# Delta-net mixer: squared norms of queries and keys as column sums on TensorE

## The chip, the cores and the metric

The kernel runs on one core of a Trainium2 chip. Five engines with queues of their own work side by side: TensorE (PE, with its weight loads listed apart as PEld), VectorE (DVE), ScalarE (ACT), GpSimd (POOL) and SyncE (SP), which here issues DMAs. The metric is the device time of one execution in microseconds; less is better.

## What is computed

The program is a trunk of two layers. Layer 0 mixes with a gated delta net and layer 1 with retention, and each has a convolutional feed-forward block behind it. The change is in the delta net alone. There are 8 heads with 128 features each, 1024 tokens, chunks of 64 tokens in the reference.

```python
qkv = jax.nn.silu(causal_dwconv(qkv, conv_w))
q, k, v = jnp.split(qkv, [H * dk, 2 * H * dk], axis=-1)
q = _l2norm(_chunk_heads(q, H, C)) * (dk ** -0.5)      # x * rsqrt(sum(x*x) + 1e-6)
k = _l2norm(_chunk_heads(k, H, C))
...
kb = k * beta[..., None]
kk = jnp.where(strict, jnp.einsum('bhncd,bhnmd->bhncm', kb, k) * decay, 0.0)
...
sol = lax.linalg.triangular_solve(kk + eye, rhs, left_side=True, lower=True, unit_diagonal=True)
...
qk = jnp.where(causal, jnp.einsum('bhncd,bhnmd->bhncm', q, k) * decay, 0.0)
...
o = o * lax.rsqrt(jnp.mean(o * o, axis=-1, keepdims=True) + 1e-6) * norm_w
```

So each token of each head needs the sum over 128 features of q squared and of k squared. The kernel never scales q and k themselves: the norm of k goes into the factors `cj` (beta over the squared norm) and `ir` (the norm), and the norm of q goes into the epsilon of the output's normalization.

## The kernel before

**Tiles.** Features lie on partitions. A tile of queries, keys or values (`feats[ti]`, with ti 0 to 7 for queries, 8 to 15 for keys, 16 to 23 for values of one head) is two halves of 128 features x 512 tokens, which take two of the 20 buffers named qkv. The kernel works in chunks of 128 tokens, eight for a head. Heads go in four pairs.

**Who fills TensorE.** In the delta-net stage, generators (`filler`, `t_path`, `t_chain`, `prep`, `dt_half`, `scan`, `tail`) yield work, and `run` chooses among them by priority with a clock of planned times: `pm` and `ptr` add a planned cost for each product, and the table `LAT` says how long after a step its result is reckoned to be there. The order on TensorE that comes out is fixed at build time (`pq` pins it). `filler` has the lowest priority: it makes the projections, 48 products of 128x512 for each half tile (`mm3` in three terms, `hT` against `wh` and `wl`), with the convolution and Silu behind them (`conv_half`, lines 446 to 459). When a tile is ready, an event `("f", ti)` is emitted at a planned time, and other streams wait for it.

**Norms of queries.** `ssq_late` starts `LAT["ssq"]` after a query tile's projections: `ssq_tile` transposes its eight 128x128 blocks on TensorE into banks of the pool acc (line 473), and ScalarE squares each block with a running sum (line 476). Line 478 adds the epsilon.

**Norms of keys.** `t_path` makes, for each head and half, four Gram blocks k k^T in one bank of the pool mm. The squared norms are their diagonals: VectorE multiplies each block with the unit matrix and sums (line 776), then adds the epsilon (779), inverts (780), multiplies by beta (781), and scales the blocks into U (line 786). After the second half POOL takes the square root `ir` (line 783). U then goes to the solve by columns on VectorE (lines 794 to 811), and from there through `t_chain` to `scan`.

**Pools.** PSUM has four banks acc, two banks mm (`mm_tile`, for all that is short-lived) and two banks sc (for the scan). A bank of mm that isn't read yet stops TensorE at the next request but one. The buffers `cv` (four) serve the convolution and the squares. Values are scaled by `ir` in `prep` (line 913), query-key blocks by the decay in `dt_half` (line 948), and `scan` scales by `cj` (line 976).

The units of `bg_ada` (lines 206 to 234), which load modulation weights (mvw) and accumulate them on VectorE (line 216), are done one at a time between the projections.

Of the kernel before, what the change touches and what calls it, by code (L numbers as in the profile page):

```python
# [15 lines left out]
P = 128  # L16
# [17 lines left out]
def trunk_kernel(ctx: ExitStack, tc, A):  # L34
# [8 lines left out]
    BUFS = {"hTa": 8, "hTb": 8, "qkv": 20, "aux": 4, "auh": 8, "lane": 4, "cv": 4, "ada": 1,  # L43
            "wr": 2, "wh": 2, "wl": 2, "t2": 3, "sm": 14, "sm2": 6, "st": 8, "s8": 6, "S": 4, "qx": 3, "fs": 1, "xT": 4}

# [417 lines left out]

    def ssq_tile(ti, tr):
        o = feats[ti]
        r = ssq[ti] = ct(f"ssq{ti}", [P, NCH])
        for half in range(2):
            pt = acc_tile()
            sq = tl("cv", [P, 516], name="sq")
            for c in range(4):  # L470
                cs = slice(c * P, (c + 1) * P)
                tr(pt[:, cs], o[half][:, cs])
            for c in range(4):
                n = half * 4 + c
                cs = slice(c * P, (c + 1) * P)
                act.activation(sq[:, cs], pt[:, cs], AF.Square, accum_out=r[:, n:n + 1])
        if ti < GH:
            dve.tensor_scalar(r, r, 1e-6, 1e-6 * P, ALU.add, ALU.mult)
        else:
            dve.tensor_scalar(r, r, 1e-6, None, ALU.add)  # L480

# [267 lines left out]
    def t_path(p):  # L749
# [12 lines left out]
        for hh, h in enumerate(heads):  # L762
            yield after_ev(("f", GH + h))
            sk = tl("sm", [P, NCH], name="sk")
            cj[h] = tl("sm", [P, NCH], name="cj")
            ir[h] = tl("sm", [P, NCH], name="ir")
            for q4 in range(2):
                yield LAT["kk"]
                pt = mm_tile()
                for c in range(4):  # L770
                    ks = fx(GH + h, q4 * 4 + c)
                    pm(pt[:, c * P:(c + 1) * P], ks, ks)
                for c in range(4):
                    n = q4 * 4 + c
                    junk = tl("S", [P, P], name="jk")
                    dve.scalar_tensor_tensor(junk, pt[:, c * P:(c + 1) * P], 1.0, ident, ALU.mult, ALU.mult,
                                             accum_out=sk[:, n:n + 1])
                qs = q4s(q4)
                dve.tensor_scalar(sk[:, qs], sk[:, qs], 1e-6, None, ALU.add)
                dve.reciprocal(cj[h][:, qs], sk[:, qs])  # L780
                dve.tensor_tensor(cj[h][:, qs], cj[h][:, qs], beta[:, qs, h], ALU.mult)
                if q4:
                    pool.tensor_tensor(ir[h], sk, phalf, ALU.pow)
                for c in range(4):
                    n = q4 * 4 + c
                    dve.scalar_tensor_tensor(U[h][:, n], pt[:, c * P:(c + 1) * P], cj[h][:, n:n + 1],
                                             U[h][:, n], ALU.mult, ALU.mult)
            for b in range(4):
                bs = slice(32 * b, 32 * b + 32)
                act.activation(X[bs, :, hh * 8:hh * 8 + 8].rearrange("p i c -> p c i"), U[h][bs, :, bs], AF.Copy)  # L790
# [246 lines left out]

    def ssq_late(ti):
        yield LAT["ssq"]
        ssq_tile(ti, ptr)  # L1040
        emit(("f", ti), 1.0)

    def filler(items):
        for kind, ti in items:
            if kind == "h":
                if ti > 1:
# [4 lines left out]
                    first_out(ti, 1, acc)  # L1051
                if first[ti] < GH:
                    yield [(0.2, ssq_late(first[ti]))]
# [21 lines left out]
            if kind == "c":  # L1075
                if ti < GH:
                    yield [(0.2, ssq_late(ti))]
# [834 lines left out]
```

## Time and profile before

| what | value |
|---|---|
| timed runs, median (lowest to highest) | 3035.81 us (3035.24 to 3036.67) |
| the profiled execution, from its first to its last instruction | 3033.2 us |
| granted TensorE clock, mean over the span | 0.977 |
| delta-net stage with the projections | about 86 to 640 us of the span |
| transposes for the norms of queries (line 639, into acc) | 64 records, median 272 ns |
| Gram blocks and query-key blocks (line 636, mm<-qkv) | 256 records, median 275 ns |
| products with the unit matrix (line 776) | 64, median 286 ns |

A row of a timeline gives the start, the time from start to end in us, the engine, the line, the operation with its output and inputs, and a count of records that were merged. In square brackets stands how long the engine was idle before it and what ended that. Records of TensorE overlap, so a product's cost in a dense stretch is the distance from start to start, not its duration. A product of 128x128 blocks in full precision stands as two records, a transpose as one. A row of a line lists the least, median and longest duration in ns.

### The profile page before, as it was taken

Reading aid. Unit: us, or ns where it says so; the run is one execution under the profiler, and the core shown is the slowest. Engines: PE = TensorE matmul, PEld = TensorE weight load, DVE = VectorE, ACT = ScalarE, POOL = GpSimd, SP = SyncE. Lnnn points to the kernel's source line nnn. Section 1 sums busy time; section 2 is a strip of 40 time slices with the busy share of each in tenths; the row PEclk is TensorE's granted clock in tenths of the full one; section 3 lists DMA queues with packets and bytes.
Section 4 is the critical chain, followed back from the end, with each engine's and each line's share of the span. In section 5 each row is a group of like instructions: output and inputs, shape, how many; then the busy total and the mean of one; then the engine's idle time right before and its main releaser. Section 6 shows DMA issues by size and latency. Waiting matters only on the chain.

```text
span 3033.2 us, 39037 instructions
## 1 busy us (share of the span) xinstructions
PE 2841.1 (94%) x13590; PEld 2309.7 (76%) x13590; DVE 2303.6 (76%) x3971; ACT 1314.4 (43%) x2408; POOL 671.3 (22%) x637
## 2 busy tenths in 40 slices
PE   8999899999999999998999999999998899999996
PEld 7877777877778888776777787767776678887885
DVE  5878788565888888988688645666788887777988
ACT  4745555434544444535333342222344544444442
POOL 0312211043021111820023302432200011113604
PEclk9999999999999999999999999999999999999998
DMA  7231222254354445854322544656654243335663
GB/s 275 78 122 53 77 84 78 88 176 144 107 169 149 148 150 170 316 176 154 132 100 89 174 163 138 209 178 178 214 199 150 90 144 104 105 105 202 238 192 122
DMA packets 243028, 450.23 MB, mean 148 GB/s; under 512 B 22928, under 2 KB 76432, under 8 KB 242832
## 3 DMA queue, kind: packets, MB, share of 16 engines
q1 hardware_dynamic: 211648, 400.02, 40.2%
q10 hardware_dynamic: 29760, 43.00, 3.9%
q0 software_dynamic: 1424, 4.72, 0.4%
q8 instruction: 107, 1.75, 0.2%
q14 instruction: 89, 0.73, 0.1%
HBM read 339.13 MB, written 108.53 MB: 148 GB/s over the span
## 4 chain that ended last, share of the span: by engine, by line
PE 55%; DVE 22%; DMA 11%; issue 6%; ACT 4%; POOL 2%; SPq 0%; POOLq 0%; DVEq 0%; ACTq 0%
PE acc L636 11%; PE acc L1148 7%; PE acc L110 4%; PE acc L111 4%; PE acc L112 4%; PE sc L636 4%; PE sc L1148 3%; DMA mvw<-in_ada_w 2%; PE acc L278 2%; PE acc L279 2%; PE acc L280 2%; PE mm L636 2%; DMA wr<-in_ffn_up 2%; DVE qkv L457 2%; DVE wb L90 2%
## 5 line engine op out<-in xcount | busy, mean ns | idle before, releaser
L636 PE MATMUL acc<-hT,wh 128*128 128x512 f32 x960 | 299.4, 393 | 0.0
L1546 POOL TENSOR_TENSOR o<-o 128x512 f32<-128x512 f32 x88 | 118.0, 1352 | 721.5 <-DVE o L1539 680.5
L278 PE MATMUL acc<-bb,ab 128*128 128x512 f32 x504 | 190.5, 406 | 33.5 <-DVE ab L90 20.4
L1148 PE MATMUL acc<-T,wb 128*128 128x512 f32 x840 | 206.0, 393 | 10.3 <-DVE wb L90 10.0
L279 PE MATMUL acc<-bb,ab 128*128 128x512 f32 x504 | 204.5, 406 | 8.8 <-DVE bb L90 8.5
L636 PEld LDWEIGHTS acc<-hT,wh 128*128 128x128 f32 x960 | 181.8, 189 | 34.1
L89 ACT ACTIVATE ab<-ar 128x512 fp32r<-128x512 f32 x210 | 128.6, 624 | 168.0 <-PE acc L280 83.7
L636 PE MATMUL acc<-hT,wl 128*128 128x512 f32 x480 | 201.2, 419 | 0.1
L280 PE MATMUL acc<-bb,ab 128*128 128x512 f32 x504 | 200.9, 400 | 0.0
L1148 PEld LDWEIGHTS acc<-T,wb 128*128 128x128 f32 x840 | 157.9, 189 | 48.4 <-DVE wb L90 14.7
L90 DVE TENSOR_TENSOR ab<-ar,ab 128x512 fp32r<-128x512 f32 x210 | 167.9, 809 | 34.5 <-ACT ab L89 34.1
L90 DVE TENSOR_TENSOR wl<-wr,wh 128x1024 fp32r<-128x1024 f32 x85 | 108.7, 1279 | 97.2 <-ACT wh L89 96.4
L90 DVE TENSOR_TENSOR wb<-wr,wb 128x512 fp32r<-128x512 f32 x162 | 114.5, 709 | 87.7 <-ACT wb L89 85.2
L90 DVE TENSOR_TENSOR wb<-mm,wb 128x512 fp32r<-128x512 f32 x216 | 145.0, 683 | 17.5 <-ACT wb L89 15.6
L89 ACT ACTIVATE wh<-wr 128x1024 fp32r<-128x1024 f32 x101 | 106.8, 1059 | 111.2 <-PE acc L636 43.4
L89 ACT ACTIVATE wb<-mm 128x512 fp32r<-128x512 f32 x216 | 122.8, 594 | 66.6 <-DVE mm L1194 65.5
L1205 ACT ACTIVATE pc<-acc 128x512 f32<-128x512 f32 x143 | 84.4, 592 | 147.1 <-PE acc L1148 92.5
L278 PEld LDWEIGHTS acc<-bb,ab 128*128 128x128 f32 x504 | 96.9, 194 | 62.5 <-DVE ab L90 20.3
L1525 DVE SCALAR_TENSOR_TENSOR o<-g,vc,o 128x512 f32<-128x512 f32 (+2 forms) x176 | 136.6, 795 | 5.1 <-ACT o L1520 4.5
L636 PE MATMUL acc<-wh,hT 128*128 128x512 f32 x384 | 137.2, 420 | 2.0 <-DVE vv L90 2.0
L89 ACT ACTIVATE wb<-wr 128x512 fp32r<-128x512 f32 x162 | 98.8, 626 | 87.0 <-DMA wr<-in_ffn_up 47.2
L216 DVE SCALAR_TENSOR_TENSOR ada<-mvw,e,ada 128x512 f32<-128x512 f32 x140 | 107.7, 769 | 29.0 <-DMA mvw<-in_ada_w 28.7
(636 smaller groups left out, 7855.7 us busy)
## 6 DMA issues: line engine op xcount, KB each, us to landing
wr<-in_ffn_up SPq DMA_DIRECT2D x96, 512.0 KB, 4.2
mvw<-in_ada_w SPq DMA_DIRECT2D x80, 512.0 KB, 4.3
ad<-o SPq DMA_DIRECT2D x154, 256.0 KB, 2.6
ar<-ad SPq DMA_DIRECT2D x154, 256.0 KB, 4.3
Br<-in_ffn_down SPq DMA_DIRECT2D x88, 256.0 KB, 3.7
wr<-in_ret_wv SPq DMA_DIRECT2D x32, 512.0 KB, 3.6
ar<-od SPq DMA_DIRECT2D x56, 256.0 KB, 5.3
xs<-xt ACTq DMA_DIRECT2D x24, 512.0 KB, 3.9
```

Source lines behind the costliest of these rows:

```text
L89: act.activation(dst_h, src, AF.Copy)
L90: eng.tensor_tensor(dst_l, src, dst_h, ALU.subtract)
L110: mm(acc, wl[:, k], hl[0], start=first, stop=False)
L111: mm(acc, wh[:, k], hl[1], start=False, stop=False)
L112: mm(acc, wh[:, k], hl[0], start=False, stop=last)
L278: mm(acc, a[1][:, sl], w[0], start=first, stop=False)
L279: mm(acc, a[0][:, sl], w[1], start=False, stop=False)
L280: mm(acc, a[0][:, sl], w[0], start=False, stop=last)
L636: pq(pe.matmul(out, lhsT, rhs, start=start, stop=stop), cost)
L1148: return pe.matmul(*a, skip_group_check=True, **kw)
L1525: dve.scalar_tensor_tensor(tv, gv[:, c0 - j:c1 - j], w[:, 2 - j:3 - j], tv, ALU.mult, ALU.add)
L1546: pool.tensor_tensor(o[d], o[x], o[y], op)
```

## The change

`ssq_tile` now serves keys as well as queries. For each half, ScalarE squares the 128x512 features in one instruction, and TensorE multiplies each block of 128 tokens, as the stationary operand, with a single column of ones. The sum over features of each token lands in one column of a bank of the pool mm, eight columns for a tile. For a query VectorE adds the epsilon as before. For a key it adds the epsilon, inverts and multiplies by beta, and POOL takes the root, once for the whole tile. The transposes, the products with the unit matrix and the small operations in `t_path` go. Key tiles now pass through `ssq_late`, which for keys waits also for the event `("g",)` of the gates (beta must be there); so `("f", ti)` of a key is emitted later than the 2.85 us that it was planned with before. The sums get a planned cost of 0.06, and `sm` has 16 buffers in place of 14.

```diff
-            "wr": 2, "wh": 2, "wl": 2, "t2": 3, "sm": 14, "sm2": 6, "st": 8, "s8": 6, "S": 4, "qx": 3, "fs": 1, "xT": 4}
+            "wr": 2, "wh": 2, "wl": 2, "t2": 3, "sm": 16, "sm2": 6, "st": 8, "s8": 6, "S": 4, "qx": 3, "fs": 1, "xT": 4}
...
-    def ssq_tile(ti, tr):
+    def ssq_tile(ti, mm):
         o = feats[ti]
         r = ssq[ti] = ct(f"ssq{ti}", [P, NCH])
+        pt = mm_tile()
         for half in range(2):
-            pt = acc_tile()
             sq = tl("cv", [P, 516], name="sq")
+            act.activation(sq[:, 0:HALF], o[half], AF.Square)
             for c in range(4):
-                cs = slice(c * P, (c + 1) * P)
-                tr(pt[:, cs], o[half][:, cs])
-            for c in range(4):
-                n = half * 4 + c
-                cs = slice(c * P, (c + 1) * P)
-                act.activation(sq[:, cs], pt[:, cs], AF.Square, accum_out=r[:, n:n + 1])
+                mm(pt[:, half * 4 + c:half * 4 + c + 1], sq[:, c * P:(c + 1) * P], ones[:, 0:1])
         if ti < GH:
-            dve.tensor_scalar(r, r, 1e-6, 1e-6 * P, ALU.add, ALU.mult)
-        else:
-            dve.tensor_scalar(r, r, 1e-6, None, ALU.add)
+            dve.tensor_scalar(r, pt[:, 0:NCH], 1e-6, 1e-6 * P, ALU.add, ALU.mult)
+            return
+        h = ti - GH
+        dve.tensor_scalar(r, pt[:, 0:NCH], 1e-6, None, ALU.add)
+        cj[h] = tl("sm", [P, NCH], name="cj")
+        ir[h] = tl("sm", [P, NCH], name="ir")
+        dve.reciprocal(cj[h], r)
+        dve.tensor_tensor(cj[h], cj[h], beta[:, :, h], ALU.mult)
+        pool.tensor_tensor(ir[h], r, phalf, ALU.pow)
...
             yield after_ev(("f", GH + h))
-            sk = tl("sm", [P, NCH], name="sk")
-            cj[h] = tl("sm", [P, NCH], name="cj")
-            ir[h] = tl("sm", [P, NCH], name="ir")
...
-                for c in range(4):
-                    n = q4 * 4 + c
-                    junk = tl("S", [P, P], name="jk")
-                    dve.scalar_tensor_tensor(junk, pt[:, c * P:(c + 1) * P], 1.0, ident, ALU.mult, ALU.mult,
-                                             accum_out=sk[:, n:n + 1])
-                qs = q4s(q4)
-                dve.tensor_scalar(sk[:, qs], sk[:, qs], 1e-6, None, ALU.add)
-                dve.reciprocal(cj[h][:, qs], sk[:, qs])
-                dve.tensor_tensor(cj[h][:, qs], cj[h][:, qs], beta[:, qs, h], ALU.mult)
-                if q4:
-                    pool.tensor_tensor(ir[h], sk, phalf, ALU.pow)
...
     def ssq_late(ti):
+        if ti >= GH:
+            yield after_ev(("g",))
         yield LAT["ssq"]
-        ssq_tile(ti, ptr)
+        ssq_tile(ti, lambda o, l, r: pm(o, l, r, cost=0.06))
         emit(("f", ti), 1.0)
...
-                if first[ti] < GH:
+                if first[ti] < 2 * GH:
                     yield [(0.2, ssq_late(first[ti]))]
...
-                if ti < GH:
+                if ti < 2 * GH:
                     yield [(0.2, ssq_late(ti))]
```

The first place is on TensorE, early in the stage, where the last decay products of the first head pair (gm against m_lowr) lie among projections (acc from hT and the weights wl and wh); cst is the unit matrix of a transpose. Before:

```order
L636 MATMUL mm<-gm,m_lowr 128x512 x2
L636 MATMUL acc<-hT,wl 128x512
L636 MATMUL acc<-hT,wh 128x512 x2
L636 MATMUL acc<-hT,wl 128x512
L636 MATMUL acc<-hT,wh 128x512 x2
L636 MATMUL acc<-hT,wl 128x512
L636 MATMUL acc<-hT,wh 128x512 x2
L639 MATMUL acc<-cst,qkv 128x128 x8
```

And with the change, from the decay product before it on (sq are the squares, ones the column):

```order
L638 MATMUL mm<-gm,m_lowr 128x512 x2
L638 MATMUL mm<-ones,sq 128x1 x16
L638 MATMUL acc<-hT,wl 128x512
L638 MATMUL acc<-hT,wh 128x512 x2
L638 MATMUL acc<-hT,wl 128x512
L638 MATMUL acc<-hT,wh 128x512 x2
L638 MATMUL acc<-hT,wl 128x512
L638 MATMUL acc<-hT,wh 128x512 x2
L638 MATMUL mm<-gm,m_lowr 128x512 x2
L638 MATMUL acc<-hT,wl 128x512
L638 MATMUL acc<-hT,wh 128x512 x2
L638 MATMUL mm<-ones,sq 128x1 x8
```

The two key tiles of the pair come in as sixteen sums in one go, right behind a decay product, and the query tile's eight transposes become eight sums; all of them now take banks of mm.

The second place is on VectorE, where the Gram blocks of the first pair are scaled into U. Before, one half of a head:

```order
L776 SCALAR_TENSOR_TENSOR jk,sk<-mm,cst 128x128 x4
L457 SCALAR_TENSOR_TENSOR qkv<-raw,vc,qkv 128x512
L779 TENSOR_SCALAR sk<-sk 128x4
L780 RECIPROCAL cj<-sk 128x4
L781 TENSOR_TENSOR cj<-cj,beta 128x4
L786 SCALAR_TENSOR_TENSOR U<-mm,cj,U 128x128 x4
```

With the change, both heads' factors, which stand ahead of all four halves:

```order
L477 TENSOR_SCALAR ssq_988<-mm 128x8
L216 SCALAR_TENSOR_TENSOR ada<-mvw,e,ada 128x512
L480 RECIPROCAL cj<-ssq_988 128x8
L481 TENSOR_TENSOR cj<-cj,beta 128x8
L477 TENSOR_SCALAR ssq_1008<-mm 128x8
L480 RECIPROCAL cj<-ssq_1008 128x8
L481 TENSOR_TENSOR cj<-cj,beta 128x8
```

The products with the unit matrix are gone, the three small operations are done once for a head, and behind them the scaling (now line 774) follows its Gram blocks directly.

## Prediction

> **What bounds the kernel now.** I read the page's totals first, then the busy time by stretches, then the list of who waited for whom. The delta-net stage, the only one that the change touches, runs from about 86 us to 640 us. The next rows give each engine's busy time with its count of instructions, in the order PE, weight loads (PEld), DVE, ACT, POOL, and then the granted clock.
>
> ```profile
> PE 2841.1 (94%) x13590; PEld 2309.7 (76%) x13590; DVE 2303.6 (76%) x3971; ACT 1314.4 (43%) x2408; POOL 671.3 (22%) x637
> ...
> 86.00:206.00 120.00, 120.00 (x565) 100.11 (x564) 100.43 (x224) 77.41 (x151) 33.63 (x47) 1.00 0.32 102
> 206.00:282.00 76.00, 65.50 (x546) 56.43 (x545) 51.89 (x173) 30.24 (x59) 16.18 (x18) 0.89 0.21 75
> 282.00:640.00 358.00, 334.37 (x2366) 284.14 (x2365) 258.94 (x665) 188.74 (x438) 63.28 (x102) 0.98 0.27 87
> ```
>
> Up to 206 us TensorE never stops: 120.00 of 120.00. From there to 640 us it stands for 10.5 + 23.6 = 34.1 us (76 - 65.50 and 358 - 334.37), at a clock that is sometimes halved: 0.89 over 76 us and 0.98 over 358 us mean 0.11 x 76 + 0.02 x 358 = 15.5 us of lost clock. VectorE is at 84% in the first stretch and about 70% later. So the stage is bound by TensorE's work, with a pool of 34.1 + 15.5 = 49.6 us that could be won back. What fills the pool is in the list of TensorE's waits (us in total, times, longest):
>
> ```profile
> PE mm L639 <- DVE DT L948: 9.4, 5, 3.5
> PE sc L636 <- ACT w L976: 7.7, 7, 1.8
> PE mm L636 <- DVE qkv L913: 3.7, 2, 3.1
> PE sc L636 <- DVE Sn L984: 3.6, 5, 1.7
> PE acc L639 <- ACT qkv L458: 2.4, 1, 2.4
> PE mm L636 <- DVE U L786: 1.7, 3, 1.0
> PE sc L636 <- DVE u L971: 1.7, 4, 0.6
> ```
>
> The largest, 9.4 + 3.7 us, are PSUM banks of the pool mm that TensorE wants again while VectorE is late in reading them. They lie where a head pair's solve ends on VectorE and ScalarE. TensorE's order is fixed when the program is built, so a late reader stops all that is queued behind, the projections included.
>
> **What leaves TensorE, and what comes.** In the trace a transpose is one record of weight load and one of matmul. Eight of them, in a stretch of dense products:
>
> ```profile
> 107.19 1.03 PEld L639 LDWEIGHTS acc<-cst,qkv 128*128 128x128 f32 x8
> 107.42 1.03 PE L639 MATMUL acc<-cst,qkv 128*128 128x128 f32 x8
> 108.18 0.30 PEld L636 LDWEIGHTS mm<-gm,m_lowr 128*128 128x128 f32 x2
> ```
>
> The load after them starts at 108.18, so a tile's eight transposes cost 108.18 - 107.19 = 0.99 us, and the eight query tiles give back 7.9 us. A column sum is not new in this kernel: line 515 makes 14 of them, with data as the stationary operand and one column of ones moving, just as the change does.
>
> ```profile
> L515 PEld LDWEIGHTS mm<-ones,mva x28: 188/192/333, 29.4 to 65.6; 128*128 128x128 f32 x28
> L515 PE MATMUL mm<-ones,mva x28: 164/250/352, 29.5 to 65.6; 128*128 128x1 f32 x28
> ...
> 43.02 1.08 PEld L515 LDWEIGHTS mm<-ones,mva 128*128 128x128 f32 x8
> 43.24 0.95 PE L515 MATMUL mm<-ones,mva 128*128 128x1 f32 x8
> 43.94 1.05 PEld L529 LDWEIGHTS mm<-cst,xt 128*128 128x128 f32 x8
> ```
>
> Fourteen sums stand as 28 records, so each is done in two passes, each with a full weight load. Eight records take 43.94 - 43.02 = 0.92 us: 0.115 us each, 0.23 us a sum, however narrow the output is. A tile has eight sums, 16 records, 1.84 us. Sixteen tiles (eight of queries, eight of keys) cost 29.4 us. **TensorE's work rises by 29.4 - 7.9 = 21.5 us.** The planner's cost of 0.06 a sum is a quarter of this, so the plan doesn't see it. The ends for this price: if only one pass of each sum cost anything, 14.7 - 7.9 = +6.8 us; at the doubled durations of a halved clock (333 ns in the row above against 188), 58.9 - 7.9 = +51 us. I take the warm row, which is the same operation with the same operands and types.
>
> **What leaves VectorE.** For each half of a key tile it now makes four products with the unit matrix and three small operations before it can scale the Gram blocks:
>
> ```profile
> 243.34 0.29 DVE L776 SCALAR_TENSOR_TENSOR jk<-mm,cst 128x128 f32<-128x128 f32 x1 [1.24 <-PE mm L636]
> ...
> 244.19 0.69 DVE L922 TENSOR_TENSOR U<-mm,eg 128x512 f32<-128x512 f32 x1
> 244.80 0.16 DVE L779 TENSOR_SCALAR sk<-sk 128x4 f32<-128x4 f32 x1
> 244.99 0.18 DVE L780 RECIPROCAL cj<-sk 128x4 f32<-128x4 f32 x1
> 245.20 0.17 DVE L781 TENSOR_TENSOR cj<-cj,beta 128x4 f32<-128x4 f32 x1
> 245.40 1.13 DVE L786 SCALAR_TENSOR_TENSOR U<-mm,cj,U 128x128 f32<-128x128 f32 x4
> ```
>
> The four products run from 243.34 to 244.19, where another operation begins: 0.85 us, 0.21 us each; the three small ones take 245.40 - 244.80 = 0.60 us. Sixteen halves make 23.2 us; the same three operations for each of eight whole key tiles come back, 4.8 us. VectorE loses 18.4 us, 4.6 us a head pair, and each Gram bank of pool mm is released 1.45 us sooner. None of this is on TensorE, so it is worth only what it takes out of the waits above.
>
> **ScalarE** turns a query tile's 16 short instructions into two squares of 128x512, and gets two such squares for each key tile:
>
> ```profile
> 110.43 0.26 ACT L476 ACTIVATE sq<-acc 128x128 f32<-128x128 f32 x1
> ...
> 112.43 0.65 ACT L452 ACTIVATE raw<-acc 128x512 f32<-128x512 f32 x1
> ...
> L783 POOL TENSOR_TENSOR ir<-sk,phalf x8: 1637/1643/1667, 133.2 to 495.6; 128x8 f32<-128x8 f32 x8
> ```
>
> From 110.43 to 112.43 is 2.0 us a query tile, 16 us in all. A 128x512 activation like the one at 112.43 takes 0.65 us; 32 of them make 20.8 us. The 4.8 us more are hidden: ScalarE is busy 188.74 us of 358. But the sums now wait for Silu and then Square, where the transposes waited for Silu alone, and the one wait of that kind before was the 2.4 us (ACT qkv L458). They also take banks of the two-buffer pool mm instead of acc. Both new waits are bounded by rows: below by -2.4 us, if that wait goes and none comes, above by some 2.4 us at several of the 15 places. I take +2. POOL's square root moves ahead to right behind a sum; POOL is busy 63.28 us of 358 and the next Gram decay products on it are needed some 15 projection products later, so it costs nothing, or, where POOL falls behind, its 1643 ns a key tile (the last row above), 13 us for all eight. SP's loads change places by one or two around the stores of Ld; I price that at nothing, since a load that came late for it would show as a wait for a weight tile, and the list above has none.
>
> **What is won back.** The listing shows that the order on TensorE hardly moves: the decay and Gram products of the first two pairs stand where they did, with sums put in between. By the first solve's end, six sum tiles have replaced two transposed ones, so TensorE arrives there 6 x 1.84 - 2 x 0.99 = 9.1 us later, and VectorE has 4.6 us less to do. The waits at that place are 3.07 us and shorter ones, and they are followed by a halved clock:
>
> ```profile
> 210.08 1.16 PE L636 MATMUL mm<-qkv 128*128 128x128 f32 x8 [3.07 <-DVE qkv L913]
> ...
> 207.88 1.54 DVE L216 SCALAR_TENSOR_TENSOR ada<-mvw,e,ada 128x512 f32<-128x512 f32 x2 [3.85 <-DMA mvw<-in_ada_w]
> ...
> 316.48 0.66 PE L639 MATMUL mm<-cst,qkv 128*128 128x128 f32 x4 [2.81 <-DVE DT L948]
> ...
> 451.85 0.66 PE L639 MATMUL mm<-cst,qkv 128*128 128x128 f32 x4 [3.48 <-DVE DT L948]
> ...
> 208.00:210.00 2.00, 0.00 (x0) 1.00 0.36 139
> 210.00:212.00 2.00, 1.35 (x9) 0.82 0.66 229
> 212.00:214.00 2.00, 2.00 (x7) 0.50 0.70 205
> ```
>
> A reader that is late by 3 us is no longer late when TensorE comes 9 us after. But part of the lateness moves with TensorE: VectorE waits there 3.85 us for a load of modulation weights (the row at 207.88), whose buffers come free only as the projections go on. I take 9 of the 13.1 us, 2 us of the Gram bank waits (L786 and its neighbours), and 3 us of clock that is no longer lost behind them: 14 of the pool's 49.6 us. The scan's own waits (w, Sn, u: 13 us) are short round trips that nothing here shortens.
>
> **The clock.** In the row for 212 to 214 us the granted clock is 0.50 after 3 us without work. That one-column products may not count as work is shown at the start of the kernel: line 515's loads take 188 to 192 ns warm and 333 ns at first, when TensorE had been busy with one-column products for 23 us on end.
>
> ```profile
> 6.40:30.00 23.60, 22.98 (x107) 1.00 1.04 392
> ...
> L157 PE MATMUL acc<-cT,mvw x64: 341/352/371, 6.4 to 20.1; 128*128 128x1 f32 x64
> ```
>
> The clock column says 1.00 there, but 352 ns against 164 to 250 ns is half speed, so I go by the durations. The place with two sum tiles in a row has 3.7 us of such products. A halving of some 4 us loses 2 us; I take one, with the wait for a bank between the two tiles, as +1. The Trainium skill, "TensorE: Matmul & The Clock Gate", Part 1, says that a busy window of about 3.4 us releases the throttle; by it sums that keep TensorE busy would hold the clock up, and this +1 would be 0. The 23 us at half speed speak against that reading.
>
> **Sum.** +21.5 (sums less transposes) + 2 + 1 - 14 = +10.5 us. The profiled span is 3033.2 us and the median of the timed runs is 3035.81 us, so 2.6 us lie around the span; they stay. 3035.8 + 10.5 = **3046.3 us**. A run of this kernel can be told from no change at about 0.2%, 6.1 us: below 3029.7 is faster, above 3041.9 slower.
>
> **Rivals.** *VectorE and ScalarE set the pace (faster).* Then the sums fall into time in which TensorE stood anyway. For: every large wait has VectorE at its end. Against: the first 120 us show none, and six of the sixteen sum tiles lie there. It decides once more than 21.5 + 3 + 6.1 = 30.6 of the 49.6 us come back; at 34 the time is 3026. Chance 0.11. *The gains balance the sums*: 18.4 to 30.6 us come back; 24.5 gives 3036, no change. The cheap end of the price (+6.8, 3032 us) lies here too. Chance 0.26. *Nothing is won back*, since loads and scan waits move along with TensorE: +21.5 + 3, 3060 us; or sums halve the clock at five of the 15 places for 4 us, 10 us more than forecast, 3056 us. Together 0.20. *The change doesn't do what it says*: the listing has 128 one-column products and no transposes into acc, so I give that nothing. The forecast, 3042 to 3055, has 0.43.
>
> The range is 3030 to 3062: its low end leaves out most of the faster case, its high end the dear price and both bad cases together. Slower 0.63, same 0.26, faster 0.11.
>
> **What would show it.** Groups of one-column products with 256 records of loads at a spacing near 0.115 us; TensorE's busy time in the stage up by some 20 us; the waits for DT L948 and qkv L913 down to about 4 us; VectorE down by 18 us. It is wrong if sums stand at 0.06 us a record, if TensorE's waits fall by more than 25 us, or if waits for Square or for banks exceed 5 us.

## The result, and the profile after

The changed kernel takes **3077.53 us** (median of 4 runs, 3075.6 to 3079.4), beside 3036.24 us for the kernel before (3035.24 to 3039.49): 1.0127 times as long, with a 95% interval of 1.0115 to 1.0139. The forecast was 3046.3 us in a range of 3030 to 3062. The direction was right, the size was not: +38.6 us by that ratio (41.3 between the medians) in place of +10.5.

The page's line of busy time of the changed kernel (its profiled span is 3074.1 us), with busy time, share of the span and count of instructions:

```profile
PE 2877.4 (94%) x13782; PEld 2343.6 (76%) x13782; DVE 2291.6 (75%) x3819; ACT 1316.1 (43%) x2312; POOL 676.5 (22%) x637
```

TensorE is busy 2877.4 - 2841.1 = 36.3 us longer, and idle 3074.1 - 2877.4 = 196.7 us where it was 192.1. VectorE is busy 12.0 us less, where the forecast had 18.4, and that shows up nowhere as time. TensorE's busy time is longer where its clock was halved, so I split it: the span is cut into windows of 2 us, and in each the busy time x (1 - granted clock) counts as lost to the halved clock. What remains of the busy time is called work at full speed.

| us, whole profiled span | before | changed | difference | forecast |
|---|---|---|---|---|
| TensorE's work at full speed | 2783.6 | 2806.1 | +22.5 | +21.5 |
| lost to the halved clock | 57.4 | 71.3 | +13.9 | +1 new, -3 won back |
| TensorE idle | 192.2 | 196.7 | +4.5 | +2 new, -11 won back |

The first row is right and the other two are wrong in their sign. The price of the sums first; group rows of the changed kernel (records, shortest/median/longest ns, first and last start), then a stretch of the timeline:

```profile
L638 PEld LDWEIGHTS mm<-ones,sq x256: 186/192/338, 107.6 to 601.2; 128*128 128x128 f32 x128
L638 PE MATMUL mm<-ones,sq x256: 164/250/354, 107.9 to 601.3; 128*128 128x1 f32 x128
```

```profile
107.86 1.84 PE L638 MATMUL mm<-ones,sq 128*128 128x1 f32 x16
109.57 0.47 PE L638 MATMUL acc<-hT,wl 128*128 128x512 f32 x1
```

There are 256 records, and a tile of 16 holds TensorE from 107.86 to 109.57, 1.7 us, a little less than the 1.84 us that the column sums of line 515 gave. Now the list of TensorE's waits from 66 to 690 us (us in total, times, longest), against the list in the prediction:

```profile
PE mm L638 <- DVE qkv L901: 7.0, 3, 2.8
PE mm L641 <- DVE DT L936: 5.6, 2, 4.7
PE sc L638 <- DVE u L959: 4.8, 6, 2.4
PE sc L638 <- ACT w L964: 4.7, 5, 1.8
PE mm L638 <- ACT sq L470: 3.5, 1, 3.5
PE sc L638 <- DVE Sn L972: 3.4, 5, 0.8
...
PE mm L638 <- DVE U L748: 1.6, 1, 1.6
```

Lines 936 and 901 are the old 948 and 913. Together they were 13.1 us and are 12.6: nothing was won back. The prediction had a reader that is 3 us late no longer late when TensorE comes 9 us after. At the first solve's end, the place of its rows at 207.88 and 210.08, the changed kernel shows this (VectorE's load, then TensorE's two waits):

```profile
222.51 1.54 DVE L216 SCALAR_TENSOR_TENSOR ada<-mvw,e,ada 128x512 f32<-128x512 f32 x2 [3.25 <-DMA mvw<-in_ada_w]
224.71 1.59 PE L638 MATMUL mm<-qkv 128*128 128x128 f32 x8 [2.20 <-DVE qkv L901]
230.98 1.12 PE L641 MATMUL mm<-cst,qkv 128*128 128x128 f32 x4 [4.68 <-DVE DT L936]
```

TensorE comes to the same product 14.6 us later (224.71 beside 210.08, where the prediction had 9.1), and the load of modulation weights lets VectorE go on 14.6 us later too (222.51 beside 207.88). So the reader is late again.

New are 3.5 us for a square and 1.6 us for a bank of mm. And the clock, in windows around one late sum tile (length, busy time, granted clock, share of DMA, GB/s), with the same place in the timeline:

```profile
498.33:501.74 3.41, 3.41 (x17) 1.00 0.44 163
501.74:505.16 3.42, 3.42 (x45) 1.00 0.70 220
505.16:508.57 3.41, 3.41 (x16) 0.50 0.40 159
508.57:511.98 3.41, 3.41 (x32) 0.50 0.26 77
511.98:515.40 3.42, 3.42 (x11) 0.50 0.00 0
515.40:518.81 3.41, 3.41 (x23) 1.00 0.00 0
```

```profile
501.62 2.17 PE L638 MATMUL mm<-T,U 64*64 64x64 f32 x32
503.72 2.29 PE L638 MATMUL mm<-ones,sq 128*128 128x1 f32 x16
505.87 1.09 PE L641 MATMUL mm<-cst,qkv 128*128 128x128 f32 x4
```

By the profile TensorE didn't stop for an instant there, and yet the clock is halved from 505.16 on: 64-column products and one-column sums filled the window before. The Trainium skill, "TensorE: Matmul & The Clock Gate", Part 1, has the clock follow the activity in a free-running window of 3413 ns. The grid of 3.41 us agrees with the trace. That busy time alone keeps the clock up doesn't: the window from 501.74 was busy from end to end.

### The profile page after: what moved, and what is told of

Its sections match the earlier page's. It is cut to its first block, busy times and chain, and to the rows that moved or that the text cites. A ratio compares the mean times of both kernels' runs of the same rounds, so it can differ in the third digit from the quotient of the medians.

```text
span 3074.1 us, 39159 instructions
## 1 busy us (share of the span) xinstructions
PE 2877.4 (94%) x13782; PEld 2343.6 (76%) x13782; DVE 2291.6 (75%) x3819; ACT 1316.1 (43%) x2312; POOL 676.5 (22%) x637
## 4 chain that ended last, share of the span: by engine, by line
PE 65%; DVE 17%; DMA 7%; issue 5%; ACT 4%; POOL 1%; SPq 0%; POOLq 0%; DVEq 0%; ACTq 0%
PE acc L638 15%; PE acc L1138 7%; PE acc L110 4%; PE acc L111 4%; PE acc L112 4%; PE sc L1138 4%; PE mm L638 3%; PE sc L638 3%; PE acc L278 3%; PE acc L279 3%; PE acc L280 3%; DVE wb L90 2%; PE sc L110 2%; PE sc L111 2%; PE sc L112 2%
## 5 line engine op out<-in xcount | busy, mean ns | idle before, releaser
L638 PEld LDWEIGHTS acc<-hT,wh 128*128 128x128 f32 x960 | 183.7, 191 | 34.6
L457 DVE SCALAR_TENSOR_TENSOR qkv<-raw,vc,qkv 128x512 f32<-128x512 f32 x144 | 110.8, 774 | 39.6 <-ACT qkv L455 38.8
```

Source lines behind the costliest of these rows:

```text
L638: pq(pe.matmul(out, lhsT, rhs, start=start, stop=stop), cost)
```

## The experiments

Each kernel was compared with runs of the kernel before beside it on the same chip, on which that kernel took 3036 to 3040 us in the median, with single runs from 3026 to 3050. A single profile is therefore uncertain by some 10 us, and the verdicts rest on the ratios; "difference" is (ratio - 1) x 3036 us, by which the change itself is +38.6. The diffs show the lines that matter; the rest of each edit is left out.

| run | ratio (95%) | difference, us |
|---|---|---|
| keys_only | 1.0114 (1.0093 to 1.0135) | +34.6 |
| queries_only | 1.0068 (1.0044 to 1.0091) | +20.6 |
| spread_sums | 1.0175 (1.0159 to 1.0190) | +53.1 |
| no_sums_const | 1.0061 (1.0040 to 1.0082) | +18.5 |
| wide_sums | 1.0121 (1.0089 to 1.0153) | +36.7 |
| f32r_sums | 1.0060 (1.0041 to 1.0079) | +18.2 |
| honest_cost | 1.0118 (1.0084 to 1.0151) | +35.8 |
| late_keys | 1.0047 (1.0029 to 1.0064) | +14.3 |
| no_diagonal | 1.0001 (0.9985 to 1.0017) | +0.3 |
| f32r_own_buffers | 1.0041 (1.0026 to 1.0055) | +12.4 |
| before_own_buffers | 0.9988 (0.9973 to 1.0003) | -3.6 |
| same_plan | 1.0192 (1.0173 to 1.0211) | +58.3 |
| same_plan_f32r | 1.0153 (1.0130 to 1.0175) | +46.5 |
| queries_same_plan | 1.0024 (1.0010 to 1.0039) | +7.3 |
| queries_same_plan_f32r | 0.9996 (0.9980 to 1.0012) | -1.2 |
| plan_kept | 1.0081 (1.0063 to 1.0098) | +24.6 |
| plan_kept_f32r | 1.0036 (1.0023 to 1.0049) | +10.9 |
| best_try | 0.9978 (0.9964 to 0.9992) | -6.7 |

**First: which half?** One half of the change at a time, and the sums spread out.

```diff
 # keys_only: queries as before
+        if ti < GH:
+            ssq_q(ti, ptr)
+        else:
+            ssq_tile(ti, lambda o, l, r: pm(o, l, r, cost=0.06))
 # queries_only: keys as before, no key in ssq_late
+        ssq_tile(ti, lambda o, l, r: pm(o, l, r, cost=0.06))
 # spread_sums: four bursts of two
+            for c in range(0, 4, 2):
+                yield 0.8
+                pt = mm_tile()
+                for j in range(2):
+                    mm(pt[:, j:j + 1], sq[:, (c + j) * P:(c + j + 1) * P], ones[:, 0:1])
```

keys_only:

> Key norms as column sums, query norms by the transposes of the kernel before. Theory W (the sums' own 1.84 us a tile, and the clock that falls to half around them): eight sum tiles add 8 x 1.84 = 14.7 us of TensorE work and half of the 13.7 us of clock, some 7, so about 3036 + 22 = 3058 us, and the two halves of the change together (with queries_only) give the whole +41. Rival V (what my forecast held: VectorE's relief takes the waits at the solves' ends away): all of the relief, 18 us of VectorE, is in this half, so it should stand near 3036 + 14.7 - 14 = 3037 us. Rival K (the key sums' place in the order and their waits are what costs, not the sums as such): nearly all of the +41 is here, 3075 us.

queries_only:

> Query norms as column sums, key norms from the Gram diagonal as in the kernel before. Theory W: 8 x (1.84 - 0.99) = +6.8 us of work and half of the clock, some 7: about 3050 us. Rival V: no relief of VectorE here, so this half alone is slower by 6.8 us or more, 3043 to 3050, and keys_only by no more than it. Rival K: next to nothing, 3037 to 3043 us.

spread_sums:

> The changed kernel, with the eight sums of a tile in four bursts of two, each in a bank of its own and with projection products between the bursts; the planner is told 0.23 us a sum. The work on TensorE is the same. Theory C (the bursts of one-column products, not their work alone, bring the half clock): time at half clock falls from 65 us to the 34 of the kernel before or less, 3077.5 - 10 to 14 = 3064 to 3068 us. Rival (the clock falls because of the waits ahead of the sums, or the sums' work alone is dearer than I think): no change, 3074 to 3080 us.

keys_only is where rival K had it (3076 us beside 3075), but queries_only isn't (3058, where K had 3043 at most), and nothing else fits. The halves add up to +55 where the whole is +38.6, and the spread sums are slower, not faster. The work at full speed was as forecast in each profile (+15.9 for the keys against 14.7, +6.9 for the queries against 6.8); the rest was clock and idle time: 16.8 + 11.3 us for the keys, 13.9 + 4.0 for the queries, 22.9 + 8.2 with the sums spread. So there is a cost which isn't the sums' work, which each half has for itself, and which spreading doesn't cure. (spread_sums also tells the planner 0.23 us a sum, and so changes the order.)

**Second: the sums themselves.** They are left out, given more columns, or halved. Without the sums the norms are left out too. A first version of that, no_sums, put squares in place of the norms; its solve goes to nonfinite numbers, and it has no time. wide_sums takes two banks of mm for a tile in place of one.

```diff
 # no_sums_const
-                mm(pt[:, half * 4 + c:half * 4 + c + 1], sq[:, c * P:(c + 1) * P], ones[:, 0:1])
+        dve.tensor_scalar(r, sq[:, 0:NCH], 0.0, 1e3, ALU.mult, ALU.add)
 # wide_sums
+                mm(pt[:, c * P:(c + 1) * P], sq[:, c * P:(c + 1) * P], ones)
 # f32r_sums: sq and onesr in F32R, two columns
+                mm(pt[:, 2 * n:2 * n + 2], sq[:, c * P:(c + 1) * P], onesr)
 # honest_cost
-        ssq_tile(ti, lambda o, l, r: pm(o, l, r, cost=0.06))
+        ssq_tile(ti, lambda o, l, r: pm(o, l, r, cost=0.23))
```

no_sums_const:

> The changed kernel with the squares but without the column sums; constants stand for the norms (the small operations read columns of a square tile, times zero), so the norms are left out. TensorE has neither sums nor transposes, VectorE all of its relief. Theory P (the order of before has its waits where they are cheap, and any shift of the events brings more windows at half clock, +14 to +23 us in all three variants so far, sums or none; VectorE's relief is worth nothing): full-speed work 8 us below before, clock 10 us above, about 3036 - 8 + 10 = 3038 us. Theory S (the half clock comes from the sums themselves): no extra half clock here, 3036 - 8 = 3028 us. Rival V (the relief is worth its 14 us when no sums stand against it): 3014 us.

wide_sums:

> The changed kernel, each sum with all 128 columns of ones as its moving operand, so that the same sums, at the same places, stream 128 columns a record instead of one; a half tile's four sums fill one bank of mm. A 128-column record stands every 0.12 to 0.13 us where a one-column record stands every 0.115, so TensorE's work is up by some 2 to 3 us. Theory S (one-column records do not count as work for the clock): the half-clock stretches that hold sums (119.5 to 129.7, 474 to 484, 505 to 515 and part of 334 to 341, 601 to 607 us in the changed kernel) go or get shorter, half-clock time in the stage from 65 to some 40 us, 3077.5 + 2.5 - 10 = about 3070 us. Theory P (the shifted events do it, sums or none): half-clock time stays near 65 us and the time at 3077 to 3083 us.

f32r_sums:

> The changed kernel with the squares and the ones in float32r, two columns of ones a sum. If a sum is then one record of load and one of product at 0.115 us, 128 records go and the sums cost 14.7 us less work; at half of the burst's length theory S has less half clock too, some 5 us: about 3077.5 - 14.7 - 5 = 3058 us. Theory P: 3077.5 - 14.7 = 3063 us or a few us around it. If the type changes nothing in the two passes: 3077 us.

honest_cost:

> The changed kernel, the planner told 0.23 us a sum (what the trace shows) instead of 0.06. TensorE does the same work; only the order is planned with the sums' real length. Theory P (the time hangs on where the waits fall in the order): another time by 5 us or more in either direction, with full-speed work the same within 2 us, and the difference in clock and idle time. Theory S, and a kernel that is indifferent to its order: 3074 to 3081 us.

Without a single sum, and with 7.8 us less work at full speed than before, the kernel is still 18.5 us slower. That was the turning point: whatever costs here, it isn't the sums alone. The clock isn't theirs alone either: the profile of no_sums_const has 13.3 us more lost to the halved clock and 11.2 us more idle than before, with no one-column sum in it, where the changed kernel has 13.9 and 4.5. wide_sums shows what the one-column records do to the clock. Two stretches, of the changed kernel and then of wide_sums:

```profile
110.00:134.00 24.00, 22.43 (x102) 0.79 0.28 98
500.00:520.00 20.00, 20.00 (x134) 0.74 0.31 106
```

```profile
110.00:134.00 24.00, 21.75 (x125) 1.00 0.29 104
500.00:520.00 20.00, 19.68 (x158) 1.00 0.30 107
```

With 128 columns in each sum the half clock is gone at both places (0.79 and 0.74 become 1.00), and 7.8 us of lost clock in the whole span. But idle time rose by 4.7 us, and one wait is new, for a bank of sums that VectorE hasn't read, at two banks a tile:

```profile
PE mm L637 <- DVE ssq L473: 6.0, 2, 5.7
```

The ratio is 1.0121 against 1.0127, with an interval of 9.7 us to either side. So one-column records do bring some half clock, more than my +1; what it costs in time wide_sums can't tell, since its edit brought a wait of nearly the same size. f32r_sums has one record a sum:

```profile
L640 PE MATMUL mm<-onesr,sq x128: 164/250/373, 108.3 to 581.3; 128*128 128x2 f32 x128
```

Half the records, 15.7 us less work, 20 us less time. honest_cost is another order with the same sums; its time isn't another one by 5 us, as theory P (the order costs) had expected, but the same (+35.8). So a true cost in the planner isn't the remedy by itself, and this run alone speaks for a kernel that is indifferent to its order.

**Third: VectorE's relief, and the loads.**

```diff
 # no_diagonal: before, constants for the key norms
-                    dve.scalar_tensor_tensor(junk, pt[:, c * P:(c + 1) * P], 1.0, ident, ALU.mult, ALU.mult,
-                                             accum_out=sk[:, n:n + 1])
+                    dve.tensor_scalar(sk, pt[:, 0:NCH], 0.0, 1e3, ALU.mult, ALU.add)
 # own buffers
-            wr = tl(bg_tag[0], [P, 2, HALF], name="mvw")
+                wr = [tl("xT", [P, HALF], name="mvw") for _ in range(2)]
```

no_diagonal:

> The kernel before without the unit-matrix products of the key norms: constants stand for the key norms, with three small operations a key tile, so the norms of the keys are left out, and VectorE has the relief of the change (18 us) with the plan of before and nothing added to TensorE. Theory M (the waits at the solves' ends move with TensorE and the loads, so the relief is worth little): 3031 to 3037 us. Rival V (my 14 us): 3020 to 3024 us. Theory R' (the relief itself moves VectorE's order so that waits get worse): above 3042 us.

f32r_own_buffers:

> The float32r version, in which the modulation loads (ada_w) have buffers of their own, those of the transposed input that are dead by then, in place of the two that they share with the weight tiles. Theory L (VectorE is late at the solves' ends because it stands in its queue for these loads, which wait for a shared buffer): the waits for DT and qkv at 218 to 224 us (5.1 us) and their half clock go, and others like them: 3054 - 8 = 3046 us or less. Rival (VectorE is late there for its own work): 3052 to 3056 us.

before_own_buffers:

> The kernel before with the same buffers for the modulation loads. Theory L: the 3.1 us wait at 207 us and the half window behind it go, some of the 9.4 us for DT too: 3036 - 5 = 3031 us or less. Rival (VectorE is late for its own work, or the loads come no earlier): 3034 to 3038 us.

The page's line and TensorE's largest waits (66 to 650 us) of no_diagonal:

```profile
PE 2844.9 (94%) x13590; PEld 2313.2 (76%) x13590; DVE 2286.2 (75%) x3819; ACT 1313.9 (43%) x2408; POOL 675.2 (22%) x637
```

```profile
PE mm L636 <- DVE qkv L909: 7.2, 2, 5.8
PE sc L636 <- ACT w L972: 5.8, 6, 1.8
PE sc L636 <- DVE u L967: 4.7, 6, 2.4
PE acc L639 <- ACT qkv L458: 3.9, 1, 3.9
...
PE acc L636 <- ACT sq L476: 2.3, 1, 2.3
PE mm L636 <- DVE DT L944: 2.0, 1, 2.0
...
PE mm L639 <- DVE DT L944: 1.1, 2, 0.8
```

This kernel leaves the norms of the keys out. VectorE has 17.4 us less to do, the planned products stand on TensorE in the order of before, and the ratio is 1.0001 (-4.6 to +5.2 us). The waits for DT fell from 9.4 to 3.1 us; the one for qkv rose from 3.7 to 7.2, u from 1.7 to 4.7, and the two for ScalarE before and behind the transposes (qkv L458 and sq L476) from 2.4 to 6.2 us. The waits change their names, and TensorE's idle time from 66 to 690 us is what it was (42.7 us before, 42.2 here).

Theory L, that VectorE is late because it waits for loads of modulation weights, is right at the first solve's end. There TensorE's waits fall from 4.6 us in the kernel before (3.07 for qkv, 0.57 and 0.94 for DT) to 1.7 us with the loads' own buffers (0.33 and 1.35), and from 5.09 us in f32r_sums to 0.60 in its version. The first row is of before_own_buffers, the second of f32r_own_buffers:

```profile
208.79 1.16 PE L642 MATMUL mm<-qkv 128*128 128x128 f32 x8 [0.33 <-DVE qkv L919]
218.03 1.16 PE L646 MATMUL mm<-qkv 128*128 128x128 f32 x8 [0.60 <-DVE qkv L909]
```

In time the buffers are worth 3.6 us on the kernel before, with an interval that reaches 1.0003, and some 6 us on the float32r version, where the intervals overlap: a gain isn't shown by either alone.

**Fourth: the order.** First the kernel before, with nothing but the later events of the keys.

```diff
 # late_keys: before, no instruction added
+    def key_late(ti):
+        yield after_ev(("g",))
+        yield LAT["ssq"]
+        emit(("f", ti), 1.0)
```

late_keys:

> The kernel before with one thing of the change alone: the planner learns that a key tile is ready as late as in the changed kernel (after the gates, 9.30 + 1.0 us behind the tile instead of 2.85). No instruction is added or removed. Theory P (the plan of before puts its waits where they are cheap, and the later key events of the change alone take it apart): half clock and idle time up as in the run without sums, 3036 + 10 to 24 = 3046 to 3060 us, with full-speed work as before. Rival R (the events are harmless; what costs is the squares on ScalarE or the missing work on VectorE): 3032 to 3040 us.

It costs 14.3 us (8.8 to 19.4), with not one instruction more. The order is the same up to a scan of the second head pair. There the four Gram blocks of a half of head 5 (second row of each pair, two records a block) come 5.1 us after the Gram blocks ahead of them in the kernel before, and 13.3 us after them, 28 rows of the timeline later, in late_keys (second pair):

```profile
356.07 1.16 PE L636 MATMUL mm<-qkv 128*128 128x128 f32 x8 [1.00 <-DVE U L786]
361.17 1.06 PE L636 MATMUL mm<-qkv 128*128 128x128 f32 x8
```

```profile
357.61 1.16 PE L636 MATMUL mm<-qkv 128*128 128x128 f32 x8 [1.01 <-DVE U L786]
370.91 1.06 PE L636 MATMUL mm<-qkv 128*128 128x128 f32 x8
```

From there on much of the order is another one: of the stage's 4243 planned products, followed one by one, at least 373 change their place among the others, most of them in projections and scans. The order on VectorE, ScalarE and GpSimd changes with it. So late_keys prices the whole order that the later events bring, and not the block of head 5 alone.

Head 5 belongs to the third pair, whose solve on VectorE can't start before this block. That solve's 31 steps (first and last start) in the kernel before, in late_keys and in the changed kernel:

```profile
L802 DVE TENSOR_TENSOR fs<-Y,T x31: 184/360/424, 376.4 to 435.8; 128x31 f32<-128x31 f32 x2, 128x60 f32<-128x60 f32 x2, 128x87 f32<-128x87 f32 x2, 128x112 f32<-128x112 f32 x2
```

```profile
L802 DVE TENSOR_TENSOR fs<-Y,T x31: 183/357/426, 386.5 to 440.7; 128x31 f32<-128x31 f32 x2, 128x60 f32<-128x60 f32 x2, 128x87 f32<-128x87 f32 x2, 128x112 f32<-128x112 f32 x2
```

```profile
L790 DVE TENSOR_TENSOR fs<-Y,T x31: 184/359/420, 401.7 to 456.3; 128x31 f32<-128x31 f32 x2, 128x60 f32<-128x60 f32 x2, 128x87 f32<-128x87 f32 x2, 128x112 f32<-128x112 f32 x2
```

It starts 10.1 us later in late_keys and 25.3 us later in the changed kernel, whose projections are only some 19 us late there. But its last step starts only 4.9 us later in late_keys (440.7 beside 435.8), so the late solve isn't shown to be the way in which the 14 us arise. If the order costs, putting it back must help. same_plan gives each sum a planned cost and time at which all 4243 other products stand exactly as before.

```diff
 # same_plan (and its f32r version)
-        if ti >= GH:
-            yield after_ev(("g",))
-        yield LAT["ssq"]
-        ssq_tile(ti, lambda o, l, r: pm(o, l, r, cost=0.06))
-        emit(("f", ti), 1.0)
+        yield LAT["ssq" if ti < GH else "fv"]
+        ssq_tile(ti, lambda o, l, r: pm(o, l, r, cost=0.109 if ti < GH else 0.0))
+        emit(("f", ti), 1.0 if ti < GH else 0.0)
 # queries_same_plan (and f32r): queries_only with
+        ssq_tile(ti, lambda o, l, r: pm(o, l, r, cost=0.109))
 # plan_kept (and f32r): same_plan with
+        yield 2.85 if ti - GH in [5] else 9.3
```

(In same_plan and plan_kept the small operations that need beta move back into `t_path`.)

same_plan:

> The changed kernel with the plan of the kernel before: a query tile's sums are planned at the cost of the eight transposes, a key tile's at nothing and 2.85 us behind the tile, as the key's event was before. All other products of the stage then stand on TensorE in exactly the order of the kernel before, with the sums put in between. Theory P (of the 41 us, 21.5 are the sums' work and the rest is the order that the later events made): 3037 + 21.5 = 3058 us, give or take 4. Theory S (the sums bring the half clock wherever they stand): full-speed work the same, clock 8 to 14 us more, 3066 to 3072 us. Neither (order and sums have little to do with the rest): 3077 us.

same_plan_f32r:

> The same with float32r sums (one pass, two columns): work up by 16 x 0.92 - 7.9 = 6.8 us. Theory P: 3037 + 6.8 = 3044 us. Theory S, at half the burst's length: 3048 to 3052 us.

queries_same_plan:

> queries_only with the sums of a tile planned at the cost of the eight transposes, so that all other products stand in the order of the kernel before. Same work as queries_only, which took 3058 us. Theory P: 3037 + 6.8 = 3044 us. Theory S, or waits for the squares and for banks of mm: 3052 to 3060 us.

queries_same_plan_f32r:

> The same with float32r sums: 8 x (0.92 - 0.99) = -0.6 us of work, the order of before, keys as before. Theory P: 3033 to 3040 us, no change. Theory S or waits for squares and banks: 3042 to 3050 us.

The queries agree with theory P: +7.3 and -1.2 against 6.8 and -0.6 us of work, closer than intervals of 4 to 5 us to either side can vouch for. The same work in queries_only's order, another one by a planned cost of 0.48 in place of 0.87 us a tile, costs 13 us more. In that order the Gram blocks of head 5 keep their place (in the trace of queries_only 5.1 us behind those ahead of them, 372.37 and 377.47, as before), so they aren't what costs there. The keys miss theory P by far, +58.3 and +46.5, for a reason that the waits of same_plan show in their first row:

```profile
PE mm L632 <- ACT sq L470: 29.2, 9, 7.0
```

The key sums came so early that TensorE stood 29.2 us for squares. So I asked which key tile's time matters for the order at all: by the planned order it is only tile 5, the keys of head 5. plan_kept moves the other seven back to 9.30 us.

plan_kept:

> same_plan again, where TensorE stood 29 us for squares because the key sums came 2.85 us behind their tiles. Here the key sums come 9.30 us behind, as in the changed kernel, without the wait for the gates and at a planned cost of nothing; only key tile 5, the one whose event moves a Gram block in the plan, keeps 2.85 us. All other products again stand in exactly the order of the kernel before. Theory P (beside the sums' work, the order is what costs): 3037 + 21.5 + 3 (one wait for a square) = about 3061 us, half clock and idle time within 6 us of before. Rival S (key sums bring waits and half clock even there): 3070 us or more.

plan_kept_f32r:

> The same with float32r sums, 14.7 us less work: theory P 3037 + 6.8 + 3 = 3047 us; rival S 3055 us or more. f32r_sums, the same work in the order of the changed kernel, took 3054 us.

+24.6 and +10.9 us, against 24.5 and 9.8 expected. The changed kernel differs from plan_kept in the order and hardly in the work, and takes 14.0 us more (38.6 - 24.6); late_keys, from the other side, gave 14.3. With float32r sums the same two orders differ by 7.3 us (18.2 - 10.9). So the order costs some 7 to 14 us, each figure known to 5 to 7 us.

How it costs isn't the same. (1 - mean granted clock) x span, averaged over the timed runs of a kernel, gives the time at a lowered clock: late_keys has only 2.4 us more of it than the kernel before beside it, so most of its 14.3 us is no loss of clock. plan_kept has 87.8 us (9.0 more than before) and the changed kernel 95.3, so that about half of their 14.0 us is clock, by means that are known to some 3 us. The condition that plan_kept's clock and idle time stay within 6 us of before didn't hold for the clock: its profile has 18.0 us more work, 12.3 us more lost to the clock and 3.5 us more idle. Its time came out as expected, but not from the expected parts. In plan_kept's waits the squares are still there, and one wait for qkv takes the place of several others (it is at the first solve's end, behind a load that VectorE waits 4.66 us for):

```profile
PE mm L632 <- ACT sq L470: 9.6, 5, 3.5
PE mm L632 <- DVE qkv L900: 7.1, 1, 7.1
```

**Fifth: what is left of the idea.** best_try is queries_same_plan_f32r with the loads' own buffers.

> The parts that cost nothing together: float32r sums for the queries alone in the order of before, keys by the Gram diagonal as before, and the modulation loads in their own buffers. Work is 0.6 us below before. If the two small gains are real (0.9996 and 0.9988 of the time before), 0.998 of it, some 5 us faster; if they are noise, 0.998 to 1.002.

It is 0.22% faster than the kernel before (0.9964 to 0.9992), 6.7 us: the only version of these whose interval lies below 1. It has the transposes of the queries replaced by sums of the same length, and keeps the keys' diagonal. Which of its two parts earns the gain isn't settled: each alone was within its interval of no change.

## Why the forecast was wrong

By its own steps:

- **The sums' work, +21.5:** right. +22.5 in the profile, and +7.3 against 6.8, +24.6 against 21.5 and a wait, in the runs that keep the order; the profile of plan_kept, with the same sums, has +18.0.
- **New waits, +2:** nearly right, and in the place it named. The changed kernel has 3.5 us for a square, 1.6 for a bank, 0.5 for another: 5.6 us, above the 5 that the text set as its own limit. The old wait of 2.4 us for Silu (qkv L458) is gone, so the net is +3.2.
- **The clock, +1:** too small, and its mechanism is only a part of the matter. 13.9 us more are lost to the clock; wide_sums, which streams 128 columns at the same places, loses 7.8 us less, but no_sums_const has no sums and loses 13.3 us more than before. By the Trainium skill's rule on a busy window, cited in the prediction, the term would have been 0; the window at 501.74 speaks against that reading.
- **Won back, -14:** wrong, and one of the two steps that failed. "A reader that is late by 3 us is no longer late when TensorE comes 9 us after" took VectorE's lateness as fixed in time. The prediction saw that VectorE waits for loads there, and that the loads' buffers come free as the projections go on, and counted this for a third of the waits. In the changed kernel the load comes 14.6 us later, as TensorE does, and the two waits are 12.6 us where they were 13.1. VectorE's relief by itself is worth nothing either: no_diagonal gave VectorE all of it in the old order, and the time didn't move (+0.3). The loads are shown as the reason at the first solve's end, where buffers of their own took most of the waits away; for the other waits it stays an argument.
- **The order, counted at 0:** the other step that failed. The text says that "the order on TensorE hardly moves: the decay and Gram products of the first two pairs stand where they did". That holds for the first two pairs, apart from small shifts. Behind them hundreds of products change places, from the Gram blocks of head 5 in the third pair on. late_keys, with nothing but the later key events, costs 14.3 us. The later key event was in the text on the change, and I asked of it only what TensorE does early in the stage.

The measured change is 28.1 us above the forecast (38.6 - 10.5). The 14 us that weren't won back and the 14 us of the order make this up, but that they do so to a tenth is luck: the order's price is known to some 5 us, and is 7 with float32r sums. The rival "nothing is won back" (3060 us) had the time of plan_kept, +24.6, though not its parts, of which the clock is 9 to 12 us. No case of mine had the order, and so the range ended too low.

What stays open: through which waits the other order costs its 14 us, and why as much clock is lost in no_sums_const, without sums, as in the changed kernel. The profile of late_keys shows 8.3 us more idle time, spread over the waits for qkv, w, u and Sn, and it comes from one execution, 7 us faster than that kernel's median, so the rest can't be traced in it. Nor do the parts add up as a rule: the order of queries_only costs 13 us alone, that of the keys 14, and the change with both 14. A rival that no run excludes is that the planned costs of the kernel before fit its own order so well that nearly any other order costs some 10 us, and that no single product is to blame.

## What to carry to other kernels

Where a planner sets a fixed order, compare the order over the whole stage, not its first part. Give a new instruction a planned cost that leaves the order alone: the query sums then cost about their work. But leave it where its operand is there in time: the key sums of same_plan kept the order and came too early, and cost 58 us. Before you count on a reader being in time because TensorE comes later, ask what the reader itself waits for, and whether that moves too. Time saved on an engine that TensorE waits for is worth nothing until a run without that work has shown it: here 17 us of VectorE were worth 0.

## What the runs showed of the hardware

The granted clock changes only on a grid of 3.413 us, and a half-clock stretch lasts a whole number of such steps, one to five in these traces: from 119.45 to 129.69 us it is three. A step that the profile has busy throughout with products of few columns can stand ahead of one (0.50 after the window at 501.74); with 128 columns at the same place it stayed at 1.00. At half clock a sum tile takes nearly a whole step: the double tile that starts at 118.96 us takes 6.51 us, and the clock is back one step after the step in which it ends. The step ahead of this stretch also has an idle time of 1.57 us:

```profile
116.04:119.45 3.41, 1.84 (x11) 1.00 0.05 8
119.45:122.87 3.42, 3.42 (x18) 0.50 0.82 298
122.87:126.28 3.41, 3.41 (x15) 0.50 0.48 141
126.28:129.69 3.41, 3.41 (x9) 0.50 0.24 91
129.69:133.11 3.42, 3.42 (x24) 1.00 0.09 38
```

A float32 sum over a 128x128 block with 128 columns of ones takes hardly longer than with one: a tile of eight takes 1.95 us at full clock in wide_sums (at 169.59) and 1.84 in the changed kernel (at 171.97). A float32r sum needs one record where float32 needs two.
